# Neighbourhood attention beside dense products: four units under way, a single gate tile, longer beginnings

## The chip, the cores and the metric

The kernel runs on one core of a Trainium2 chip. The metric is the device time of one execution in microseconds (us), median over the runs. The profile is of one execution on the same chip.

## The reference

One encoder layer on two sequences (1024 and 2048 tokens of 1024 features) with 16 meta tokens ahead of each. All in fp32.

```python
xn = _rmsnorm(h, g_pre)
proj = xn @ w_in + b_in                       # 1024 x 6672
na_q, na_k, na_v, na_z, ml_qk, ml_v, ml_z, ml_o, ml_g, mg = split(proj)
ya = neighbourhood_attention(na_q, na_k, na_v, na_rpb)   # 8 heads of 64, 8x16 windows on a 64-wide grid, plus meta tokens
ya = (ya * silu(na_z)) @ w_a
yb = (mlstm(ml_qk, ml_v, ml_g, ml_o, conv_w, head_g) * silu(ml_z)) @ w_b   # both directions, 4 heads of 128, head norm
ga, gb = split(sigmoid(mg))
y = (ga * ya + gb * yb) @ w_out
return h + _rmsnorm(y, g_post)
```

## The kernel before

Every fp32 product is made as three products of split operands (high by high, high by low, low by high), so most of TensorE's time goes into the dense projections, at lines 144 to 146 (512 columns wide), 394 to 396 and 1284 to 1286 (256 wide).

**Two generators.** `dense` yields the projections in pieces: groups of the input projection first, and then, for each block of 512 tokens (two of sequence 0, four of sequence 1), `final`: the products with `w_a` and `w_b` (L1258, through `mm3` at L144 to L146), gated by tiles `tg` that come from memory by DMA (L1247, multiplied in at L1263), and the product with `w_out` (L1284 to L1286). `sparse` yields, in the order mLSTM 0, attention 0, mLSTM 1, attention 1, the short dependent steps. `run` meters one against the other: after each step of `sparse`, which yields a figure in us (`A_NA` = 1.52 in attention, `A_N` = 1.85 in the mLSTM's norm), it takes so many us worth of products from `dense`:

```python
acc += w
while acc > 0.0:
    d = next(dense, None)
    if d is None or d is True:
        acc = 0.0
        break
    acc -= d
```

So a pause (`yield A_NA`) puts 1.52 us worth of products behind the step on TensorE. `dense` yields `True` while the next block is not ready, that is while its attention is not done; then the sparse steps follow one another with no product between. When `sparse` is over, what is left of `dense` runs.

**Order.** TensorE's instructions stand as they are written. On the other engines and on SP, which issues the DMAs, a scheduler sets the order; each engine then works strictly in that order.

**Attention** (`na`). For each of its heads (row block, pair `pr`, half `hh`), `na_prep` loads and splits the operands in six steps: DMAs for `qr`, `kr`, and for the first head of a pair `vr` and the gate `zt` (L613); then copies and subtractions on ScalarE and VectorE (`stk`, `qB`, `kd`, `kx`, `vt`). The first head's six steps come ahead of all scores, with one pause behind each. A head has four units `cb`. In step `u` of the loop: `na_scores` of unit u (two products into `sc` at L644 and L645, bias and maximum L648 on VectorE, exp L652 on ScalarE); pause; `na_scale` of unit u (L660, L661), and `na_out` of unit u-2 (four products of `vt` and `pts` at L681, then L685 and L687; behind the last unit of a pair the gating with `zt` at L689 and the store `ya` at L690); pause; `na_turn` of unit u-1 (four transposes at L669, then `pts` high on ScalarE, L671, and low on VectorE, L672); pause. Three units are under way at a time.

**Norm** (`ml_norm`). Loads of 256 tokens ahead (`hn`, `tog`, `szg`), statistics and normalisation on VectorE (L1158 to L1173), then transposes at L1184. One pause stands behind the first load.

**Between blocks.** `yload` reads the eight slices of the next block (`yr`, L1225: four from the attention's stores `ya`, four from the mLSTM's `yb`) and splits them into `yh` (L1227, ScalarE) and `yl` (L1228, VectorE). It is begun beside the `w_out` products of the block before as soon as the next block is ready, and at the block's start otherwise.

Of the kernel before, what the change touches and what calls it, by code (L numbers as in the profile page):

```python
# [9 lines left out]
F32 = mybir.dt.float32  # L10
F32R = mybir.dt.float32r
# [6 lines left out]
P = 128  # L18
# [30 lines left out]
def _row_types(R):  # L49

    out = []
    for t in range(R // 8):
        if t == 0:
            out.append((0, 0, 11))
        elif t == R // 8 - 1:
            out.append((2, R - 12, 12))
        else:
            out.append((1, 8 * t - 4, 15))
    return out
# [48 lines left out]
A_NA, A_D, A_A, A_N, A_G = 1.52, 1.63, 1.63, 1.85, 1.3  # L108


class K:
# [420 lines left out]
    def na(self, s, rts):  # L532

        tc, nc, i = self.tc, self.nc, self.i
        rows = _row_types(SEQLEN[s] // 64)
        with tc.tile_pool(name=f"na{s}{rts[0]}", bufs=1, side="right", reuse_waits="tile") as np_:
            self.qB = [np_.tile([P, 4, P], F32R, name=f"qB{j}") for j in range(2)]
            self.kx = [np_.tile([P, 16, 64], F32R, name=f"kx{j}") for j in range(2)]
            self.gts = [np_.tile([P, 17, 48], F32, name=f"gt{j}") for j in range(2)]
            for q in self.qB:  # L540
                nc.gpsimd.dma_start(q[64:128], i["onehot"].rearrange("a (b c) -> a b c", b=4))
            for g in self.gts:
                nc.gpsimd.memset(g[:, 0, :], 0.0)
                nc.gpsimd.memset(g[:, 16, :], 0.0)
            heads = [(rt, pr, hh) for rt in rts for pr in range(4) for hh in range(2)]
            n = len(heads)
            prep = self.na_prep(np_, s, rows, heads, 0)
            for k in range(6):
                next(prep, None)
                yield A_NA  # L550
            self.na_bias(rows, heads, 0)
            cur, nxt = self.head, None
            units = [(j, cb) for j in range(n) for cb in range(4)]
            ready = {}
            for u in range(len(units) + 2):
                if u < len(units):
                    j, cb = units[u]
                    if cb == 0:
                        cur = self.head
                        prep = self.na_prep(np_, s, rows, heads, j + 1) if j + 1 < n else iter(())  # L560
                        next(prep, None)
                    ready[u] = [cur, heads[j], cb, None, None, self.gts[j % 2]]
                    self.na_scores(np_, ready[u], rows)
                    if j + 1 < n and cb == 0:
                        self.na_bias(rows, heads, j + 1)
                yield A_NA
                if u < len(units):
                    self.na_scale(np_, ready[u])
                    if cb:
                        next(prep, None)  # L570
                if u >= 2:
                    self.na_out(np_, ready.pop(u - 2), s)
                yield A_NA
                if 1 <= u <= len(units):
                    self.na_turn(np_, ready[u - 1], rows)
                    if u < len(units) and cb >= 2:
                        next(prep, None)
                yield A_NA
# [9 lines left out]
    def na_prep(self, np_, s, rows, heads, j):  # L588

        nc, i = self.nc, self.i  # L590
        rt, pr, hh = heads[j]
        typ, lo, nr = rows[rt]
        ns, h0 = nr + 1, hh * 64
        ms, rs = ((nr, 0), (nr, 0), (0, 1))[typ]
        qr = np_.tile([P, 512], F32, name="qr", bufs=1)
        stk = np_.tile([P, 4, P], F32R, name="stk", bufs=2)
        qb = self.qB[hh]
        self.twice(qr, self.NQ[s][pr], h0, rt * 512)
        sv = stk.rearrange("p b t -> p (b t)")
        kr = np_.tile([P, 16, 64], F32, name="kr", bufs=1)  # L600
        kd = np_.tile([P, 16, 64], F32R, name="kd", bufs=2)
        kx = self.kx[hh]
        self.twice(kr[:, rs:rs + nr, :].rearrange("p a b -> p (a b)"), self.NK[s][pr], h0, lo * 64)
        self.twice(kr[:, ms, :], self.NKM[pr], h0, 0)
        ks = 8 * ns
        if hh == 0:
            self.vr = np_.tile([P, 8, P], F32, name="vr", bufs=1)
            f0 = pr * P
            nc.sync.dma_start(self.vr[ms * 8:ms * 8 + 8], self.NVM[:, f0:f0 + P].rearrange("(b c) f -> c b f", c=8))
            nc.sync.dma_start(self.vr[rs * 8:(rs + nr) * 8],  # L610
                              self.NV[s][:, lo * 8:(lo + nr) * 8, f0:f0 + P].rearrange("b q f -> q b f"))
            self.zt = np_.tile([P, 512], F32, name="zt", bufs=2)
            nc.sync.dma_start(self.zt, self.NZ[s][pr][:, rt * 512:(rt + 1) * 512])  # L613
            self.yg = np_.tile([P, 512], F32, name="yg", bufs=2)
        vr, zt, yg = self.vr, self.zt, self.yg
        if j < 2 or rows[heads[j - 2][0]][0] != typ:
            nc.gpsimd.dma_start(kx[64:128, :ns, :].rearrange("p a b -> p (a b)"), i["masks"][typ, :, :ns * 64])
        yield
        nc.scalar.activation(sv, qr, AF.Copy)
        yield  # L620
        nc.scalar.activation(qb[0:64], stk[0:64].bitcast(F32), AF.Copy)
        nc.vector.tensor_tensor(sv[64:128], qr[64:128], sv[64:128].bitcast(F32), op=ALU.subtract)
        yield
        nc.scalar.activation(kd[:, :ns, :], kr[:, :ns, :], AF.Copy)
        yield
        nc.vector.tensor_tensor(kx[0:64, :ns, :], kr[0:64, :ns, :], kd[0:64, :ns, :].bitcast(F32), op=ALU.subtract)
        vt = np_.tile([P, 8, 2, 64], F32R, name="vt", bufs=2)
        vv = vr[:ks, :, h0:h0 + 64]
        nc.scalar.activation(vt[:ks, :, 0], vv, AF.Copy)
        yield  # L630
        nc.vector.tensor_tensor(vt[:ks, :, 1], vv, vt[:ks, :, 0].bitcast(F32), op=ALU.subtract)
        self.head = stk, qb, kd, vt, yg, zt
        yield

# [28 lines left out]
    def na_turn(self, np_, unit, rows):  # L663
        nc = self.nc
        pr_, _, N = unit[3]
        ks = N // 4
        pt = self.psum("tr", [P, 4, P])
        for ch in range(4):
            nc.tensor.transpose(pt[:ks, ch, :], pr_[:, ch * ks:(ch + 1) * ks], self.ident)  # L669
        pts = np_.tile([P, 4, 2, P], F32R, name="pts", bufs=2)  # L670
        nc.scalar.activation(pts[:ks, :, 0, :], pt[:ks], AF.Copy)  # L671
        nc.vector.tensor_tensor(pts[:ks, :, 1, :], pt[:ks], pts[:ks, :, 0, :].bitcast(F32), op=ALU.subtract)  # L672
        unit[4] = pts
# [461 lines left out]
    def ml_norm(self, mp, s):  # L1135

        nc = self.nc
# [3 lines left out]
        def load(i):  # L1141
            if i < N:
                ld[i] = []
                for e in range(2):
                    rows = slice((2 * i + e) * P, (2 * i + e + 1) * P)
                    hb = mp.tile([P, 4, P], F32, name="hn", bufs=6)
                    to = mp.tile([P, 4, P], F32, name="tog", bufs=4)
                    sz = mp.tile([P, 4, P], F32, name="szg", bufs=4)
                    for x, dr in ((hb, self.H), (to, self.TO), (sz, self.SZ)):
                        nc.sync.dma_start(x.rearrange("p a b -> p (a b)"), dr[s][rows, :])  # L1150
                    ld[i].append((hb, to, sz))
# [38 lines left out]
                rr.pop(i)  # L1190

        load(0)
        yield A_N
        for i in range(N + 1):
            if i < N:
                load(i + 1)
# [272 lines left out]
```

## Time and profile before

| what | value |
|---|---|
| median of 3 runs | 2956.09 us (2948.89 to 2957.51) |
| the profiled execution | 2951.54 us, of it a span of 2949.8 us |
| TensorE busy | 2837.0 us, 96% |
| VectorE busy | 1788.2 us, 61% |
| ScalarE busy | 1322.5 us, 45% |
| mean granted clock of TensorE | 0.991 |

The span runs from the first to the last instruction. PE is TensorE, DVE is VectorE, ACT is ScalarE, SP the queue that issues the DMAs. The norm and attention stages that matter below lie at about 713 to 775 us (norm 0), 776 to 1178 us (attention 0), 1908 to 2004 us (norm 1) and 2007 to 2830 us (attention 1); the final blocks run from 2230 us on. "PE sm L681 <- DVE pts L672: 24.9, 23, 2.6" in the view of waits reads: TensorE sat idle ahead of line 681, whose output is `sm`, until VectorE's line 672 had written `pts`: 24.9 us in all, 23 times, the longest 2.6 us. A row of the windows gives the stretch, its length, the busy time and number of instructions of PE, PEld, DVE, ACT and POOL, and then TensorE's granted clock, the DMA's busy share and GB/s.

### The profile page before, as it was taken

How to read it: one execution, taken by the hardware profiler on the slowest of the kernel's cores; microseconds unless marked ns; L12 is line 12 of the kernel's file. 1: busy time of each engine (PE TensorE's matmuls, PEld its weight loads, DVE VectorE, ACT ScalarE, POOL GpSimd, SP SyncE). 2: the span in 40 equal slices, each digit the busy share in tenths (PEclk: the TensorE clock that was granted, in tenths of full speed). 3: DMA queues.
4: the chain of work that ended last, by engine and by line, in shares of the span. 5: the costliest groups of instructions: out<-in, count | busy, mean ns of one | idle time of the engine just before them, and what ended most of it. 6: DMA issues, size and time to landing. Idle time of an engine off the chain costs nothing. (4 is left out here: it accounts for less than half of the span.)

```text
span 2949.8 us, 49769 instructions
## 1 busy us (share of the span) xinstructions
PE 2837.0 (96%) x17616; PEld 2520.4 (85%) x17616; DVE 1788.2 (61%) x4818; ACT 1322.5 (45%) x3178; POOL 23.5 (1%) x111
## 2 busy tenths in 40 slices
PE   6999999999999999999999999999999989999998
PEld 6998897899799988888888988877887978888897
DVE  5233566556656764565566565495568877776853
ACT  4113545433443453455565454434455544544421
POOL 1000000000000000000000000000000000000000
PEclk9999999999999999999999999999999999999999
DMA  7555666556756563666765554496579898988875
GB/s 252 199 176 183 204 212 204 166 176 210 237 176 197 152 189 101 203 193 194 222 206 189 173 182 151 160 356 196 179 232 329 288 276 268 281 273 252 287 260 205
DMA packets 415914, 633.33 MB, mean 215 GB/s; under 512 B 51920, under 2 KB 252704, under 8 KB 415664
## 3 DMA queue, kind: packets, MB, share of 16 engines
q1 hardware_dynamic: 414544, 627.46, 66.7%
q0 software_dynamic: 1120, 2.69, 0.4%
q8 instruction: 138, 2.26, 0.3%
q14 instruction: 112, 0.92, 0.1%
HBM read 438.27 MB, written 191.74 MB: 214 GB/s over the span
## 5 line engine op out<-in xcount | busy, mean ns | idle before, releaser
L144 PE MATMUL pj<-xh,whi 128*128 128x512 f32 (+1 forms) x1824 | 722.4, 396 | 1.2 <-DVE xl L299 0.9
L145 PE MATMUL pj<-xl,whi 128*128 128x512 f32 (+1 forms) x1824 | 701.9, 385 | 0.1
L146 PE MATMUL pj<-xh,wlo 128*128 128x512 f32 (+1 forms) x1824 | 700.2, 384 | 0.0
L394 PE MATMUL pj<-whi,xh 128*128 128x256 f32 (+3 forms) x1576 | 450.9, 286 | 0.0
L395 PE MATMUL pj<-wlo,xh 128*128 128x256 f32 (+3 forms) x1576 | 444.6, 282 | 0.0
L396 PE MATMUL pj<-whi,xl 128*128 128x256 f32 (+3 forms) x1576 | 444.0, 282 | 0.0
L146 PEld LDWEIGHTS pj<-xh,wlo 128*128 128x128 f32 x1824 | 345.2, 189 | 72.3
L144 PEld LDWEIGHTS pj<-xh,whi 128*128 128x128 f32 x1824 | 345.9, 190 | 57.6 <-DVE xl L299 1.3
L145 PEld LDWEIGHTS pj<-xl,whi 128*128 128x128 f32 x1824 | 346.1, 190 | 53.7 <-DVE xl L299 0.4
L394 PEld LDWEIGHTS pj<-whi,xh 128*128 128x128 f32 (+1 forms) x1576 | 294.1, 187 | 1.2
L395 PEld LDWEIGHTS pj<-wlo,xh 128*128 128x128 f32 (+1 forms) x1576 | 293.8, 186 | 1.1
L396 PEld LDWEIGHTS pj<-whi,xl 128*128 128x128 f32 (+1 forms) x1576 | 293.9, 186 | 0.9
L1284 PE MATMUL pj<-whi,mh 128*128 128x256 f32 x768 | 220.1, 287 | 0.6 <-DVE yo L1312 0.6
L652 ACT ACTIVATE prb<-sc,mx 128x384 f32<-128x384 f32 (+2 forms) x192 | 119.5, 622 | 220.1 <-DVE mx L648 211.4
L1286 PE MATMUL pj<-whi,mlo 128*128 128x256 f32 x768 | 216.4, 282 | 0.0
L1285 PE MATMUL pj<-wlo,mh 128*128 128x256 f32 x768 | 216.2, 281 | 0.0
L672 DVE TENSOR_TENSOR pts<-tr,pts 96x512 fp32r<-96x512 f32 (+2 forms) x192 | 131.9, 687 | 120.6 <-ACT pts L671 119.6
L671 ACT ACTIVATE pts<-tr 96x512 fp32r<-96x512 f32 (+2 forms) x192 | 114.5, 596 | 153.2 <-PE tr L669 152.3
L144 PE MATMUL pj<-yh,whi 128*128 128x512 f32 x384 | 158.0, 411 | 19.8 <-DVE tg L1263 19.8
L403 DVE TENSOR_TENSOR stT<-pj,bb 128x256 f32<-128x256 f32 (+3 forms) x197 | 83.0, 422 | 123.5 <-PE pj L396 121.7
L146 PE MATMUL pj<-yh,wlo 128*128 128x512 f32 x384 | 153.0, 398 | 0.0
L145 PE MATMUL pj<-yl,whi 128*128 128x512 f32 x384 | 152.8, 398 | 0.0
(234 smaller groups left out, 5145.0 us busy)
## 6 DMA issues: line engine op xcount, KB each, us to landing
whi<-wh SPq DMA_DIRECT2D x176, 512.0 KB
wlo<-wl SPq DMA_DIRECT2D x176, 512.0 KB
wh<-whi SPq DMA_DIRECT2D x64, 512.0 KB
wl<-wlo SPq DMA_DIRECT2D x64, 512.0 KB
wraw<-w_in SPq DMA_DIRECT2D x48, 512.0 KB
gt<-st SPq DMA_DIRECT2D x96, 256.0 KB
tg<-gt SPq DMA_DIRECT2D x96, 256.0 KB
xr<-x_sample SPq DMA_DIRECT2D x24, 512.0 KB
```

The source lines that it names most:

```text
L144: mm(out, ah, bh, start=start, stop=False)
L145: mm(out, ah, bl, start=False, stop=False)
L146: mm(out, al, bh, start=False, stop=stop)
L394: nc.tensor.matmul(o, xh, wh, start=k == 0, stop=False)
L395: nc.tensor.matmul(o, xh, wl, start=False, stop=False)
L396: nc.tensor.matmul(o, xl, wh, start=False, stop=k == KT - 1)
L652: nc.scalar.activation(pr_[:, :N].rearrange("p (b a c) -> p b a c", b=4, c=8), sc[:, :N].rearrange("p (a b c) -> p b a c", b=4, c=8), AF.E ...
L671: nc.scalar.activation(pts[:ks, :, 0, :], pt[:ks], AF.Copy)
L672: nc.vector.tensor_tensor(pts[:ks, :, 1, :], pt[:ks], pts[:ks, :, 0, :].bitcast(F32), op=ALU.subtract)
L1284: nc.tensor.matmul(o, mh[:, k, xs], wh, start=k == 0, stop=False)
L1285: nc.tensor.matmul(o, mh[:, k, xs], wl, start=False, stop=False)
L1286: nc.tensor.matmul(o, ml[:, k, xs], wh, start=False, stop=k == KT - 1)
```

## The change

Four edits. `na_out` comes three steps behind the scores instead of two, and `pts` gets three buffers for it. `zt` is loaded at the end of the second head's preparation, into one buffer instead of two, and held by the head rather than by `self`. In `na`, three pauses instead of one stand behind the first step of the first preparation, which issues the loads. In `ml_norm`, four pauses instead of one stand behind the first load. The products are the same in number and order; the attention's and the norm's instructions stand at other places among them.

```diff
             for k in range(6):
                 next(prep, None)
-                yield A_NA
+                for _ in range(1 if k else 3):
+                    yield A_NA
...
-            for u in range(len(units) + 2):
+            for u in range(len(units) + 3):
...
-                if u >= 2:
-                    self.na_out(np_, ready.pop(u - 2), s)
+                if u >= 3:
+                    self.na_out(np_, ready.pop(u - 3), s)
                 yield A_NA
...
-            self.zt = np_.tile([P, 512], F32, name="zt", bufs=2)
-            nc.sync.dma_start(self.zt, self.NZ[s][pr][:, rt * 512:(rt + 1) * 512])
             self.yg = np_.tile([P, 512], F32, name="yg", bufs=2)
-        vr, zt, yg = self.vr, self.zt, self.yg
+        vr, zt, yg = self.vr, None, self.yg
...
         nc.vector.tensor_tensor(vt[:ks, :, 1], vv, vt[:ks, :, 0].bitcast(F32), op=ALU.subtract)
+        if hh:
+            zt = np_.tile([P, 512], F32, name="zt", bufs=1)
+            nc.sync.dma_start(zt, self.NZ[s][pr][:, rt * 512:(rt + 1) * 512])
         self.head = stk, qb, kd, vt, yg, zt
...
-        pts = np_.tile([P, 4, 2, P], F32R, name="pts", bufs=2)
+        pts = np_.tile([P, 4, 2, P], F32R, name="pts", bufs=3)
...
         load(0)
-        yield A_N
+        for _ in range(4):
+            yield A_N
         for i in range(N + 1):
```

## The prediction

> **What bounds the kernel now.** I read the busy shares first, then the chain of waits of TensorE, then windows around each long wait.
>
> ```profile
> span 2949.8 us, 49769 instructions
> PE 2837.0 (96%) x17616; PEld 2520.4 (85%) x17616; DVE 1788.2 (61%) x4818; ACT 1322.5 (45%) x3178; POOL 23.5 (1%) x111
> ```
>
> TensorE (PE) is the bound: 2837.0 of 2949.8 us are busy, 112.8 us idle. The change keeps every matrix product, so it can only move idle time. The profiled execution took 2951.54 us, 1.7 us beside its span, and lies 4.6 us under the median 2956.09 of the three runs; I work the sum on the profile and carry the difference to the median. A measurement of this kernel tells about 0.3% (8.9 us) from no change.
>
> The waits of TensorE over the whole span (us in total, times, longest):
>
> ```profile
> PE sm L681 <- DVE pts L672: 24.9, 23, 2.6
> PE pj L144 <- DVE tg L1263: 19.8, 7, 5.4
> PE tr L1184 <- DVE hn L1173: 5.2, 1, 5.2
> PE sc L644 <- ACT kd L624: 3.8, 1, 3.8
> PE tr L1184 <- issue: 2.8, 1, 2.8
> PE sc L645 <- DVE kx L626: 0.5, 1, 0.5
> ```
>
> The edits aim at L681 (the attention's last product waits for the turned probabilities, `pts`), at L1184 (the first transposes of a norm, twice) and at L644/L645 (first scores of an attention). The direct cause of L1263 stays: VectorE waits for the gate tiles `tg`, which come by DMA.
>
> An idle stretch costs more than itself. Windows behind such waits (the last figures of a row are granted clock, DMA share, GB/s):
>
> ```profile
> 735.00:742.00 7.00, 5.76 (x19) 4.82 (x20) 7.00 (x32) 1.19 (x2) 0.00 (x0) 0.53 0.56 191
> 786.00:793.00 7.00, 6.46 (x17) 5.05 (x17) 2.00 (x4) 1.15 (x2) 0.00 (x0) 0.51 1.03 354
> 1018.00:1021.50 3.50, 3.50 (x19) 3.49 (x19) 2.90 (x8) 1.69 (x5) 0.00 (x0) 0.52 0.00 0
> 2629.20:2632.60 3.40, 3.40 (x12) 2.70 (x11) 2.94 (x7) 1.88 (x4) 0.00 (x0) 0.50 0.89 285
> 1928.00:1935.00 7.00, 7.00 (x34) 5.70 (x33) 7.00 (x37) 1.85 (x3) 0.00 (x0) 1.00 1.03 405
> ```
>
> After the norm's 5.2 us wait (it ends at 736.2) the clock is 0.53 for 7 us: 3.3 us lost. After the first scores' 4.3 us it is 0.51 for 7 us: 3.4 us. After two of the L681 waits it is half for 3.4 to 3.5 us: 1.7 us each. After the second norm's 2.8 us wait it stayed 1.00.
>
> **The fourth unit.** `na_out` of a unit moves behind one more step of three pauses, each metered as 1.52 us of products: 4.56 us more between the write of `pts` and its use. The longest of the 23 waits is 2.6 us, so all are covered: 24.9 us, and 1.7 us of clock twice, 28.3 us. `pts` gets a third buffer; its slot is still freed one step before it is written again, so no new wait. `vt` of the head before is read one step later, which leaves one step before it is overwritten: nothing, as long as `na_out` is on time.
>
> How much is given back? Most of these waits lie beside the final blocks. The waits from 2230 to 2800 us, of TensorE and then of VectorE:
>
> ```profile
> PE sm L681 <- DVE pts L672: 19.8, 20, 2.6
> PE pj L144 <- DVE tg L1263: 17.4, 5, 5.4
> ...
> DVE tg L1263 <- DMA tg<-gt: 30.6, 21, 4.3
> ```
>
> And that stage in windows:
>
> ```profile
> 2240.00:2380.00 140.00, 131.06 (x830) 114.85 (x828) 120.23 (x266) 75.88 (x169) 0.00 (x0) 1.00 0.94 306
> 2380.00:2520.00 140.00, 127.76 (x806) 112.95 (x807) 106.57 (x251) 64.17 (x154) 0.00 (x0) 0.99 0.89 274
> 2520.00:2660.00 140.00, 127.11 (x805) 113.55 (x803) 104.20 (x247) 63.59 (x154) 1.02 (x2) 0.98 0.89 270
> 2660.00:2800.00 140.00, 135.32 (x875) 122.38 (x876) 110.75 (x268) 66.95 (x164) 0.00 (x0) 0.99 0.84 274
> ```
>
> L681 has 19.8 of its 24.9 us here, next to 17.4 us that go back to late `tg`. DMA is busy for 0.84 to 0.94, VectorE for 74% to 86%: neither is full on the mean, both are near it in bursts. A PE that waits less asks for transfers sooner. The give-back lies between 0 and all 21.5 us (19.8 and 1.7 of clock); with 6 to 16% of DMA free I take 8 us.
>
> On the clock, the Trainium skill ("TensorE: Matmul & The Clock Gate", Part 1: The HAM clock gate) says that the array falls to half rate after at least one idle window of about 3.4 us. The trace disagrees as to the length: the L681 wait ahead of the third window above was shorter,
>
> ```profile
> 1016.88 0.39 PE L681 MATMUL sm<-pts,vt 104*128 104x256 f32 x1 [2.25 <-DVE pts L672]
> ```
>
> 2.25 us. By that page the L681 waits would cost no clock, and the sum would be 3.4 us smaller. I go by the trace.
>
> **The beginnings.** A norm gets three more pauses of 1.85 us, 5.55 us of products against waits of 5.2 and 2.8 us: both go, 8.0 us, and 3.3 us of clock: 11.3. The two attentions get 3.04 us after the first loads; only the first waits there, 4.3 us: 3.0 us go, 1.3 us stay, too short to drop the clock (2.8 us did not in the second norm): 6.4 us. If transfers rather than time end these waits, the gain shrinks to nothing; that is a rival below.
>
> **The gate tile.** `zt` is loaded into one buffer at the end of the odd head's preparation instead of with the even head. On SP it can go out once the pair before has been multiplied (L689), and it stands behind that pair's store `ya`, whose wait is the same one. Its use is some seven units, about 30 us, later: nothing. If that cover were gone, L689 would hold VectorE for the load, 2.8 us by the `yr` row below (issue 2832.59, use 2835.39).
>
> **The end, where the change costs.** More pauses mean more products used up: 2x2x1.52 + 2x3x1.52 + 2x3x1.85 = 26.3 us. Before, the last attention product was followed by products in stock. The timeline of that place:
>
> ```profile
> 2824.76 0.60 PE L669 MATMUL tr<-ident,prb 128*104 128x128 f32 x4
> 2825.45 0.60 ACT L671 ACTIVATE pts<-tr 104x512 fp32r<-104x512 f32 x1 [1.62 <-PE tr L669]
> 2826.09 0.69 DVE L672 TENSOR_TENSOR pts<-tr,pts 104x512 fp32r<-104x512 f32 x1 [1.46 <-ACT pts L671]
> 2828.04 0.63 PE L681 MATMUL sm<-pts,vt 104*128 104x256 f32 x4
> 2828.51 0.28 PE L1284 MATMUL pj<-whi,mh 128*128 128x256 f32 x1
> ...
> 2829.65 0.69 DVE L689 TENSOR_TENSOR yg<-yg,zt 128x512 f32<-128x512 f32 x1
> 2830.37 0.32 SPq L690 DMA_DIRECT2D ya<-yg  x1
> 2832.59 0.32 SPq L1225 DMA_DIRECT2D yr<-ya  x1
> 2834.85 1.19 SPq L231 DMA_DIRECT2D wlo<-wl  x2
> 2835.39 0.63 ACT L1227 ACTIVATE yh<-yr 128x512 fp32r<-128x512 f32 x1 [1.92 <-DMA yr<-ya]
> 2836.06 0.69 DVE L1228 TENSOR_TENSOR yl<-yr,yh 128x512 fp32r<-128x512 f32 x1 [2.13 <-ACT yh L1227]
> 2837.15 0.42 SPq L1225 DMA_DIRECT2D yr<-yb  x1
> 2846.19 0.69 DVE L1228 TENSOR_TENSOR yl<-yr,yh 128x512 fp32r<-128x512 f32 x1 [3.70 <-ACT yh L1227]
> 2847.06 0.40 PE L144 MATMUL pj<-yh,whi 128*128 128x512 f32 x1
> 2847.30 0.39 PE L145 MATMUL pj<-yl,whi 128*128 128x512 f32 x1
> ```
>
> From 2828.51 to 2847.06 PE had 18.6 us of products, under which the last `yg` was stored, read back as `yr` and split into `yh`, `yl`. 26.3 exceeds 18.6 by 7.7 us, five pauses. The order of the changed program's instructions says the same: no product stands between the last four transposes and the last block, and the last two `na_out` stand back to back. So that chain is bare. From the transposes (time 0) `pts` is ready at 2826.78 - 2824.76 = 2.0; PE has 0.9 us of work, waits 1.1, and starts the last `na_out` at 2.0, ending at 2.5. From its start to the fourth `yl`, which is made from this store, takes 2836.75 - 2828.04 = 8.7 us: 10.7. The first three slices are ready earlier, and their nine products run meanwhile, 9 x 0.235 = 2.1 us, to 4.6: wait 6.1 us. The eighth `yr` waits for the slot of the fourth, so its `yl` comes 2.8 + 1.4 us after the fourth's, at 14.9, against twelve products from 10.7, 2.8 us: wait 1.4 us. Some Newton steps stand between on VectorE (I allow 0.5), and half clock may follow: 1.7 to 3.4 us. Lower end 1.1 + 6.1 + 1.4 + 0.5 = 9.1. Upper end: the eighth `yr` lands as late as before (2846.88 - 2828.04 = 18.8 us after the last `na_out` starts, weights were ahead of it), so 20.8 - 2.5 - 21 x 0.235 = 13.4, with 1.1 and 3.4: 17.9. In the changed order the weights go out ahead of `ya`, so I take 12, nearer the lower.
>
> **Sum.** -28.3 + 8 - 11.3 - 6.4 + 12 = -26.0 us: the profile 2951.5 becomes 2925.5, the median 2956.1 becomes 2930.
>
> **Rivals.**
> *The final blocks are full.* The 21.5 us there come back as waits for `tg`: -46.0 + 21.5 + 12 = -12.5, 2943.6. For it: DMA at 0.94. Against: 2660 to 2800 has the smallest share, 0.84, and the least idle PE. Chance 0.23.
>
> *The beginnings don't do what they say.*
>
> ```profile
> 725.00:736.50 11.50, 6.25 (x28) 4.80 (x27) 10.42 (x59) 5.39 (x10) 0.00 (x0) 0.93 1.01 383
> ```
>
> Ahead of the first norm's transposes VectorE is busy 10.42 of 11.5 us and DMA is full; added products bring their own evacuations and weights there. Then only the fourth unit counts: -28.3 + 8 + 12 = -8.3, 2947.8. Against: the wait comes once and not again in the norm. Chance 0.12.
>
> *Slower: late gate tiles multiply.* Attention shifts against the final blocks, so each head's loads meet other `tg` loads. A late one costs up to 5.4 us and 1.7 of clock, 7 us. To eat the 34 us of net gain before give-back and 8.9 more it takes over six such waits, one more in each of the six blocks; at seven, +15 us, 2971. For it: five in the stage already. Against: nothing makes them more frequent. Chance 0.13.
>
> **How the numbers follow.** The forecast keeps 0.52. Its best case is -46.0 + 9.1 = -37 us, 2919, and the runs spread 7 us below their median: 2912. Above, the range takes in the first two rivals with 5 us: 2953; it leaves out the third. Faster: 0.50 + 0.18 + 0.04 = 0.72; same 0.02 + 0.05 + 0.08 = 0.15; slower 0.13.
>
> **What would show it.** Right: L681's wait below 5 us; no wait over 2 us at L1184; a PE gap of 6 to 13 us between the last attention product and the last block, with half clock behind it; `tg` waits of 20 to 30 us. Wrong: `tg` waits over 40 us, or L681's wait turned up at L644 or L669, or an end gap over 18 us.

## The result: 0.5% slower, and the profile after

| kernel | median | runs | ratio to before (95%) |
|---|---|---|---|
| before | 2954.94 us | 4 (2948.89 to 2957.51) | |
| changed | 2970.89 us | 4 (2968.22 to 2972.52) | 1.0050 [1.0028, 1.0071] |

The changed kernel is 16 us slower; the forecast was 2930 with a range of 2912 to 2953. The profiled execution took 2972.22 us against 2951.54. Its page:

```profile
span 2970.5 us, 49826 instructions
PE 2849.1 (96%) x17616; PEld 2531.6 (85%) x17616; DVE 1790.1 (60%) x4818; ACT 1324.3 (45%) x3178; POOL 23.3 (1%) x111
```

The products are the same 17616, yet TensorE is busy for 12.1 us longer than before (2837.0), at a mean granted clock of 0.984 for 0.991, and idle for 121.4 us instead of 112.8. TensorE's waits over the whole span of the changed kernel (us in total, times, longest), those that the argument uses:

```profile
PE pj L144 <- DVE tg L1266: 18.0, 8, 4.6
PE pj L296 <- DVE xl L299: 14.9, 13, 2.9
PE pj L1289 <- DVE mlo L1270: 12.3, 5, 4.4
...
PE pj L144 <- ACT yh L1230: 6.5, 1, 6.5
PE sc L646 <- ACT kd L623: 6.0, 1, 6.0
PE tr L671 <- DVE prb L663: 5.0, 5, 1.6
...
PE sm L683 <- DVE pts L674: 1.0, 1, 1.0
```

L683 is the old L681: 24.9 us have become 1.0. The 8.0 us at L1184 are gone altogether. So of the three groups of waits that the edits aimed at two went as forecast, and the third, ahead of the first scores, did not. In their place stand L1289 (a `w_out` product waits for `mlo`, 0 before), 6.5 us at the last block's start, a longer wait ahead of the first scores (6.0 for 3.8), more at L671 (5.0 for 0.5) and, behind ScalarE's `prb`, at L646 (8.7 for 3.9), and more at L296, the transposes of the projection's input (7.6 before).

Where the time went is best read at equal products: the start of the product with the same number among those written into `pj`, in both traces, so that a stage is compared with the same stage. The gain or loss of each stage against before, in us (stages by their times in the kernel before; minus is faster):

| kernel | to 743: start, norm 0 | to 1109: attention 0 | to 1958: mLSTM 1, first half of norm 1 | to 2031: rest of norm 1 | to 2245: attention 1 alone | to 2838: beside final blocks | end | sum |
|---|---|---|---|---|---|---|---|---|
| forecast | -8.5 | -13.2 | -2.8 | 0 | 0 | -13.5 | +12 | -26.0 |
| changed | -9.9 | -5.8 | +7.3 | +4.5 | +2.8 | +7.8 | +14.0 | +20.7 |
| a1_unit | -3.6 | -5.9 | +16.4 | +6.7 | -3.3 | -3.0 | +5.0 | +12.4 |
| a2_pauses | -11.5 | -2.1 | +12.9 | -1.0 | +5.9 | +14.3 | +16.6 | +35.0 |
| a3_stock | -9.6 | -7.7 | +8.4 | +2.6 | -0.3 | -1.8 | +3.5 | -4.9 |
| a4_phase | -9.8 | -2.6 | +0.1 | -2.6 | +2.5 | -14.7 | +9.4 | -17.7 |
| b1_norm | -10.2 | -7.5 | +15.5 | +6.0 | -2.4 | -12.1 | +10.2 | -0.5 |
| b2_three | -11.5 | -2.6 | +4.2 | -0.5 | +2.3 | -10.8 | +3.6 | -15.2 |
| b3_best | -8.7 | -4.1 | -2.7 | -2.6 | -1.0 | -11.5 | +1.8 | -28.7 |
| b4_bare | -0.5 | -1.1 | +4.7 | -1.6 | +1.4 | -1.1 | +17.4 | +19.3 |
| c1_pool | -9.0 | -9.0 | +8.7 | +3.9 | -0.1 | +8.1 | +17.6 | +20.2 |
| c2_three_stock | -10.4 | -2.5 | +8.0 | -0.6 | +2.4 | -11.6 | +3.3 | -11.4 |
| c3_place | -0.8 | -0.9 | -1.6 | +2.3 | -3.0 | -17.0 | +3.6 | -17.2 |
| c4_bestpool | -9.9 | -0.2 | -1.3 | -2.6 | +2.0 | -17.1 | +1.0 | -28.0 |
| d1_nogate | -8.3 | -6.9 | +7.7 | +3.6 | +3.1 | -32.0 | +11.3 | -21.5 |
| d2_ml | +0.8 | -5.3 | +25.8 | +5.1 | -1.8 | +3.7 | +3.0 | +31.3 |
| d3_late | +0.2 | -1.7 | -1.0 | +1.1 | +6.7 | +9.2 | +1.4 | +16.0 |
| d4_place_nogate | -0.2 | -4.7 | +1.3 | -0.1 | -4.4 | -26.7 | +4.1 | -30.8 |
| d5_before_nogate | -2.4 | -2.0 | +6.4 | +2.3 | -4.6 | -26.2 | -2.9 | -29.4 |

Each row is one profiled execution; the last 69 us of attention 0 stand in the third column. How far one stage wanders by itself shows where two kernels are alike: b4_bare is the kernel before up to the last row block, and differs by 4.7 us in mLSTM 1. A single figure below 5 us is therefore not read. The changed kernel and b1_norm are alike up to norm 1, and there they agree: from 1109 to 1918 us they lose 12.1 and 14.2 us. The 8.2 us between their two figures of that stage arise in norm 1, whose pauses differ. So the changed kernel's +7.3 is 12.1 us lost before norm 1 and 4.9 gained in its first half.

Beside the final blocks the two kernels wait about equally long. The changed kernel from 2230 to 2830 us:

```profile
PE pj L144 <- DVE tg L1266: 15.7, 5, 4.6
PE pj L1289 <- DVE mlo L1270: 12.3, 5, 4.4
PE tr L671 <- DVE prb L663: 5.0, 5, 1.6
PE pj L1287 <- ACT mh L1269: 2.8, 3, 2.0
PE pj L1287 <- DVE tg L1266: 1.3, 1, 1.3
PE sc L646 <- ACT prb L654: 0.7, 1, 0.7
...
DVE tg L1266 <- DMA tg<-gt: 29.0, 24, 3.2
```

That is 37.8 us of TensorE's waits, where before had 39.4 (2230 to 2800 us), 19.8 of them at L681. VectorE's wait for gate tiles hardly moved: 29.0 us for 30.6. The clock did move. The windows of 560 us, of before and then of the changed kernel (the last three figures: granted clock, DMA share, GB/s):

```profile
2240.00:2800.00 560.00, 521.24 (x3313) 463.74 (x3312) 441.76 (x1029) 270.59 (x640) 1.02 (x2) 0.99 0.89 281
```

```profile
2240.00:2800.00 560.00, 524.65 (x3312) 470.95 (x3311) 439.15 (x1020) 270.81 (x639) 1.02 (x2) 0.97 0.90 283
```

Before's waits at L681 were 20 of 1 us on the mean; the changed kernel has the same time in 20 waits where before had 30, and its clock is 0.97. In the traces of 2230 to 2830 us the clock was half for 34.1 us, and for 13.7 before. If half of that time counts as lost, some 10 us more are lost in the changed kernel, by which an estimate of waits and clock together gives 55 us for it and 46 for before. That is near the 7.8 us that this stage lost. The same estimate gives 29 us for c3_place below (24.3 us of waits, 10.2 us at half clock), whose stage gained 17.0.

### The profile page after: what moved, and what is told of

Same layout as the page of the kernel before. It is cut to its first block, busy times and chain, and to the rows that moved or that the text cites. A ratio compares the mean times of both kernels' runs of the same rounds, so it can differ in the third digit from the quotient of the medians.

```text
span 2970.5 us, 49826 instructions
## 1 busy us (share of the span) xinstructions
PE 2849.1 (96%) x17616; PEld 2531.6 (85%) x17616; DVE 1790.1 (60%) x4818; ACT 1324.3 (45%) x3178; POOL 23.3 (1%) x111
## 4 chain that ended last, share of the span: by engine, by line
PE 77%; DMA 11%; DVE 7%; ACT 2%; issue 1%; SPq 1%; DVEq 0%; ACTq 0%
PE pj L144 13%; PE pj L145 13%; PE pj L146 13%; PE pj L394 6%; PE pj L395 6%; PE pj L396 6%; DMA tg<-gt 3%; PE pj L1289 3%; PE pj L1287 3%; PE pj L1288 3%; PE sm L683 2%; PE tr L671 2%; DMA um<-ud 2%; PE sc L646 1%; PE sc L647 1%
## 5 line engine op out<-in xcount | busy, mean ns | idle before, releaser
L144 PE MATMUL pj<-xh,whi 128*128 128x512 f32 (+1 forms) x1824 | 722.7, 396 | 1.3 <-ACT st L323 1.2
L144 PEld LDWEIGHTS pj<-xh,whi 128*128 128x128 f32 x1824 | 346.4, 190 | 58.1 <-ACT st L323 1.7
L1289 PE MATMUL pj<-whi,mlo 128*128 128x256 f32 x768 | 219.1, 285 | 12.3 <-DVE mlo L1270 12.3
L144 PE MATMUL pj<-yh,whi 128*128 128x512 f32 x384 | 160.0, 417 | 24.5 <-DVE tg L1266 18.0
L1289 PEld LDWEIGHTS pj<-whi,mlo 128*128 128x128 f32 x768 | 147.5, 192 | 13.3 <-DVE mlo L1270 13.3
```

The lines of the kernel that those rows point to most:

```text
L144: mm(out, ah, bh, start=start, stop=False)
L1289: nc.tensor.matmul(o, ml[:, k, xs], wh, start=False, stop=k == KT - 1)
```

## The experiments

In all of them "place" is how many us of products the metering has handed out when a step begins. Before, mLSTM 1 begins at 951.8 and attention 1 at 1624.9, and 18.6 us of products are left in stock when the last attention is over. In the changed kernel it is 964.5, 1643.2 and none.

**a1_unit: the fourth unit alone.** The changed kernel without the two edits of pauses:

```diff
-                for _ in range(1 if k else 3):
-                    yield A_NA
+                yield A_NA
...
-        for _ in range(4):
-            yield A_N
+        yield A_N
```

> The fourth unit (with pts in three buffers and the gate tile in one) without any of the added pauses. It uses 9.1 us more products than the kernel before, so about 10 of the 18.6 us of stock behind the last attention product stay. Theory (the end and the shifted beginnings cost, the unit alone gives nothing in the final blocks): L681's waits below 3 us, but the waits in the final blocks turn up at the w_out product that needs the last low half of m (12 us) and at the transposes (5 us); norm waits as before (8 us); end gap below 5 us; time within 6 us of before, 2949 to 2961. Rival (the deeper pipeline itself is what slows the kernel): within 4 us of the changed kernel, 2967 to 2975. My prediction's view: 20 us faster than before, 2935.

Measured: 2962.55 us (10 runs), 1.0023 [1.0008, 1.0037], just over the theory's 2961 and 27 us above the prediction's 2935. The unit moves mLSTM 1 to 956.0 and attention 1 to 1629.1; that stage lost 16.4 us. So the unit without the pauses was no gain either.

**a2_pauses: the pauses alone, three units.** The kernel before with both edits of pauses.

> The added pauses of attention and norm alone; three units as before. 17.2 us more products are used, so the stock at the end is all but gone. Theory (the end costs 11 us, the norm's waits go for 11 us): L681 waits stay near 25 us; no wait at L1184; a gap at the start of the last block of 4 to 8 us with half clock behind it; time 2952 to 2966. Rival (the pauses are harmless, the unit is what costs): 2938 to 2948.

Measured: 2986.05 us, 1.0104 [1.0076, 1.0132]. Both expectations missed: alone, the pauses cost 29 us beside a median before of 2957.1. With three units in this place L682 (the old L681) waits longer than before. From 2230 to 2850 us:

```profile
PE sm L682 <- DVE pts L673: 36.4, 19, 6.1
PE pj L144 <- DVE tg L1265: 6.6, 2, 4.8
PE tr L670 <- DVE prb L662: 2.9, 2, 1.8
```

**a3_stock: the end restored by faster attention 1.** The changed kernel with attention 1's pauses metered as 1.454, so that the stock at the end is 18.6 again.

```diff
+        a_na = (A_NA, 1.454)[s]
...
-                yield A_NA
+                yield a_na
```

> The changed kernel with the second attention's pauses metered at 1.454 us instead of 1.52, so that the stock of products at the end is again that of the kernel before (18.6 us). Theory (the bare end costs 1.0 + 6.5 us of gap and 3.4 us of half clock): the last block starts without a gap; 11 us faster than the changed kernel, 2957 to 2963. Rival (the end is only where a delay from earlier shows, because the last attention unit came late anyway): under 4 us faster, 2967 or more.

Measured: 2945.50 us, 0.9960 [0.9946, 0.9974], more than expected. The end fell from +14.0 to +3.5, as the theory had it; the final blocks fell too, by 9.6 us. The smaller pauses also move every head, which may be why; it was not tested apart.

**a4_phase: mLSTM 1 back at its place.** The changed kernel with attention 0's pauses as 1.459: mLSTM 1 begins at 951.8 as before, attention 1 at 1630.5, and TensorE has 5.8 us of products behind the last attention product (3 were expected).

```diff
+        a_na = (1.459, A_NA)[s]
...
-                yield A_NA
+                yield a_na
```

> The changed kernel with the first attention's pauses metered at 1.459 us, so that the second mLSTM begins at the same place among the products as in the kernel before; the end has 3 us of stock. Theory (the 12.8 us shift puts the transposes that build the next half beside heavier mLSTM steps): waits at L296 fall from 14.9 to about 8 us, the 12 us lost from 1484 to 1577 us don't come; 10 to 16 us faster than the changed kernel, 2955 to 2961. Rival (the transposes wait because VectorE's order is another with four units or norms, not for the place): waits at L296 stay at 13 to 16 us, time 2965 or more.

Measured: 2932.32 us, 0.9926 [0.9903, 0.9950]: 39 us below the changed kernel, with all its instructions and some shorter pauses. The theory gave 10 to 16. mLSTM 1's stage went from +7.3 to +0.1, the final blocks from +7.8 to -14.7.

**b1_norm: only attention 1 at that place.** The changed kernel with norm 1's pauses as 1.580: mLSTM 1 stays at 964.5, attention 1 begins at 1631.9.

```diff
+        a_n = (A_N, 1.580)[s]
...
-            yield A_N
+            yield a_n
```

> The changed kernel with the second norm's pauses metered at 1.580 us instead of 1.85: the second mLSTM keeps the shifted place among the products, the second attention begins within 2 us of products of where it begins in the version with the first attention metered (2932 us), and the stock at the end is the same 3 us. It parts the two shifts. Theory (each shift has its own price: 12 us at the second mLSTM, some 22 us in the final blocks): L296 waits near 15 us as in the changed kernel, final blocks as in the faster version; time 2940 to 2950. Rival (only the mLSTM's place matters, the final blocks were a matter of luck): 2955 to 2965. Other rival (only the final blocks' place matters): 2930 to 2936.

Measured: 2947.43 us, 0.9972 [0.9953, 0.9990], as the theory had it: the final blocks gain (-12.1), mLSTM 1's stage still loses (+15.5).

**b2_three: that place with three units.** The kernel before with the changed kernel's pauses, attention 0's as 1.4775: the places of a4_phase, 10 us in stock.

> Three units and the gate tile as before, the added pauses, and the first attention metered at 1.4775 us so that the second mLSTM and the second attention begin at the same place among the products as in the version at 2932 us; 10 us of stock at the end against its 3. It isolates the fourth unit at one place. Prediction's term (L681's waits and their clock are worth 28 us, 8 of it given back): 18 to 28 us slower than 2932, 2950 to 2960, L681 waits 20 us or more. Rival (in the final blocks the waits only move to the transposes and the low half of m, the unit is worth the 6 us of the first attention): 2930 to 2940.

Measured: 2936.31 us, 0.9942 [0.9921, 0.9962]. The rival was right: 2936 with three units, 2932 with four. The waits of the final blocks, 2230 to 2830 us, are about equal in sum, 25.2 us here and 24.5 in a4_phase (beside 3.9 at the start of its last block), and differ in where TensorE meets them:

```profile
PE sm L683 <- DVE pts L674: 19.8, 16, 3.1
PE pj L144 <- DVE tg L1266: 2.8, 2, 2.4
PE pj L1287 <- ACT mh L1269: 1.8, 1, 1.8
```

```profile
PE tr L672 <- DVE prb L664: 10.3, 11, 2.0
PE pj L1288 <- ACT mh L1270: 4.8, 3, 2.0
PE pj L144 <- ACT yh L1231: 3.7, 2, 3.5
PE pj L1290 <- DVE mlo L1271: 3.2, 4, 1.6
```

The first fence is b2_three, the second a4_phase.

**b3_best: a4_phase with products in stock for the end.** The last row block's pauses as 1.37, by which 21.5 us of products stand behind the last attention product (18.7 were expected):

```diff
+                    if s and heads[j][0] == 3:
+                        a_na = 1.37
```

> The version at 2932 us with the last row block's pauses metered at 1.37 us, so that 18.7 us of stock stay behind the last attention product. Theory (a bare end costs 7 to 13 us): the 9.4 us lost there don't come, 2920 to 2927, the fastest so far. Rival (the place in the last block but one counts more): 2930 or more.

Measured: 2923.52 us, 0.9896 [0.9866, 0.9926], the theory's figure and the fastest complete kernel here: 1% below the one before.

**b4_bare: the bare end alone.** The kernel before with the last row block's pauses as 1.714, so that no product is left in stock.

> The kernel before with nothing changed but the last row block's pauses, metered at 1.714 us, so that no product is in stock behind the last attention product. It measures the bare end by itself. Theory: a gap of 5 to 8 us at the start of the last block with half clock behind it, 8 to 16 us slower than before. Rival (the end hides it): within 4 us of before.

Measured: 2964.55 us, 1.0036 [1.0014, 1.0059]; 10 us slower, the end +17.4 in the profiled execution, which took 2970.88. The term of the forecast for the end is real by itself.

**c1_pool: is VectorE's burst the carrier?** The changed kernel with one line on another engine:

```diff
-                nc.vector.tensor_tensor(yl[:, k - 2], yr.pop(k - 2), ...)
+                nc.gpsimd.tensor_tensor(yl[:, k - 2], yr.pop(k - 2), ...)
```

> The changed kernel with one operation moved: the subtraction that makes yl for the next block (L1231) runs on GpSimd instead of VectorE; every instruction keeps its place among the products. It asks what carries the waits in the final blocks. Theory: bursts of VectorE do (four yl and the gating of yo stand ahead of the mlo or the turned probabilities that TensorE needs), so without yl in that queue the waits at L1289 fall from 12.3 us to under 5, those at L671 fall too, and the time is 8 to 12 us below the changed kernel: 2959 to 2963. Rival: late gate tiles or the place of the mLSTM carry the loss; then the waits change by less than 4 us in all and the time stays at 2967 or more.

Measured: 2968.94 us, 1.0045 [1.0032, 1.0057], 2 us below the changed kernel: the theory fell. From 2230 to 2830 us the waits moved again:

```profile
PE pj L144 <- DVE tg L1266: 20.9, 7, 4.7
PE pj L1289 <- DVE mlo L1270: 8.0, 4, 2.8
PE tr L671 <- DVE prb L663: 5.9, 5, 1.8
PE sc L646 <- ACT prb L654: 3.9, 4, 1.6
PE pj L1287 <- ACT mh L1269: 1.6, 1, 1.6
```

40.3 us in all. VectorE was relieved by 16.5 us only (below), so the test was weaker than meant, but what it did free bought nothing: the final blocks lost 8.1 us, as in the changed kernel.

**c2_three_stock: the fourth unit by itself at the good place.** b3_best with three units; pauses 1.4775 and, in the last row block, 1.432, give the same places and nearly the same stock (20.1 us for 21.5).

> The kernel b3_best with three units under way instead of four (and pts and zt in two buffers as before); its pauses give the same places for the mLSTM and the attention and the same stock at the end. It measures the fourth unit by itself at a good place. Theory: the unit only moves the waits of the final blocks from L681 to other lines and is worth 8 us at most: 2926 to 2932. Rival, the prediction's term (28.3 us of waits and clock gone, 8 given back): about 20 us above b3_best, 2943 or more.

Measured: 2935.28 us, 0.9945 [0.9924, 0.9965], between the two expectations: the two kernels lie 11.8 us apart. How much of it is the unit's stays open: the two traces differ most in mLSTM 1's stage (by 10.7 us), which holds no attention, and not at all beside the final blocks (-11.6 and -11.5).

**c3_place: one edit of the kernel before.** Only norm 1's three pauses: attention 1 at 1630.5, mLSTM 1 unmoved, 13 us in stock.

```diff
-        yield A_N
+        for _ in range((1, 4)[s]):
+            yield A_N
```

> The kernel before with a single edit: three more pauses in the second norm (5.55 us of products). The mLSTM keeps its place among the products, attention 1 begins 5.6 us of products later, and 13 us of products stay in stock at the end. Theory: the place of attention 1 against the final blocks is worth 13 to 15 us by itself, beside some us from the norm's wait: 2938 to 2945. Rival: the place is worth nothing and only the norm's wait of 2.8 us goes: 2950 to 2956.

Measured: 2936.25 us, 0.9937 [0.9916, 0.9959]; 19 us, slightly more than the theory gave, for 5.6 us of products moved. Apart from norm 1's 2.8 us at L1184 the waits at which the change aimed are still there. In the final blocks the gate tiles' wait at L144 is the one that went, from 17.4 to 3.3. From 2230 to 2830 us:

```profile
PE sm L681 <- DVE pts L672: 21.0, 19, 2.5
PE pj L144 <- DVE tg L1264: 3.3, 2, 3.0
DVE tg L1264 <- DMA tg<-gt: 21.8, 17, 2.7
```

**c4_bestpool: b3_best with `yl` on GpSimd.**

> The kernel b3_best with the yl subtraction on GpSimd. Theory (VectorE's bursts carry what waits are left in the final blocks, some 15 us at L671, L1287 and L1289): 2915 to 2921. Rival: at this place the bursts no longer meet TensorE, or GpSimd's longer operation delays the next block's start; then 2923 or more.

Measured: 2926.75 us, 0.9907 [0.9885, 0.9929]: no gain over b3_best. The rival held.

**d2_ml: the place of mLSTM 1 alone.** The kernel before with attention 0's pauses as 1.582 and norm 1's as 1.553: mLSTM 1 at 964.5, attention 1 at 1624.9 as before.

> The kernel before with its pauses in attention 0 stretched from 1.52 to 1.582 and those in the second norm cut from 1.85 to 1.553: mLSTM 1 begins after 964.5 us of products as in the changed kernel, attention 1 after 1624.9 as before. It measures by itself what the later place of mLSTM 1 costs. Theory: 10 to 13 us, as the transposes that build half of the input operand for its groups meet VectorE late (waits at L296 for xl over 10 us, half clock near 1510 and 1553 us): 2962 to 2968. Rival: that loss belongs to the other edits of the changed kernel; then 2953 to 2958.

Measured: 2980.32 us, 1.0085 [1.0065, 1.0105]; 25 us slower, twice what the theory gave, and not at the line that it named: TensorE waits only 3.9 us for `xl` between 1100 and 1970 us. Of the stage's 25.8 us, 20.8 were lost before norm 1 (by 1918 us in the kernel before), in several small waits and three half clocks (near 1203, 1254 and 1524 us); the rest, and the 5.1 us behind it, belong to norm 1, whose pauses are cut. That the later place costs is shown here, and by b1_norm's +15.5 beside a4_phase's +0.1; which wait carries it differs from kernel to kernel. It is not the place alone: c2_three_stock, at the old place of 951.8, lost 8.0 us in this stage.

**d3_late: attention 1 at the changed kernel's place, else as before.** Ten more pauses in norm 1, attention 1 at 1643.2; the last row block as 1.385, 14 us in stock.

> The kernel before with ten more pauses in the second norm, 18.3 us of products: attention 1 begins after 1643.2 as in the changed kernel; mLSTM 1 keeps its place and the last row block's pauses are cut to 1.385 so that 14 us of products stay in stock at the end. With c3_place (1630.5, 2936 us) and the kernel before (1624.9, 2955 us) it shows whether the place of attention 1 has a good and a bad side. Theory: 1643.2 is as bad a place as 1624.9, with 35 us or more of waits between 2230 and 2830 us, and the time is 2948 to 2958. Rival: any later place is good, and the loss of the changed kernel comes from mLSTM 1 and its bare end alone: 2932 to 2942.

Measured: 2963.98 us (10 runs), 1.0022 [1.0008, 1.0037], on the theory's side and worse, with 40.6 us of TensorE's waits from 2230 to 2830 us. So with three units 1630.5 is good (2936), 1624.9 and 1643.2 are bad (2955 and 2964): it isn't that later is better. How wide the good place is stays open: a1_unit, with four units at 1629.1, gained only 3.0 us beside the final blocks.

**d1_nogate, d4_place_nogate and d5_before_nogate: no gate loads, at three places.** The changed kernel, c3_place and the kernel before, each with one load left out:

```diff
-                    nc.sync.dma_start(tg, self.GT[s][8 * br + ft][:, t0:t0 + n])
...
-                nc.vector.scalar_tensor_tensor(ms[br], ms[br], 1.0, p, ...)
+                nc.vector.scalar_tensor_tensor(ms[br], self.gpost[:, :n], 1.0, p, ...)
```

> The changed kernel without the loads of the gate tiles tg (the gating multiplies by a tile that is in memory already, so 24 MB of loads and the gating's values are left out); all instructions of TensorE keep their places. It asks whether late gate tiles carry the waits that the final blocks have at this place. Theory: they do, as the cause behind L144 and L1289 alike, so of the 38 us of waits between 2230 and 2830 us fewer than 18 stay and the time is 15 to 25 us below the changed kernel, 2946 to 2956. Rival, the one that c1_pool leaves standing for VectorE itself (whatever is taken away, its queue is met by TensorE at another line): at least 28 us of waits stay and the time is 2962 or more.

> The kernel c3_place without the loads of the gate tiles (left out as in d1_nogate). At this place only 3 us of TensorE's waits are for tg. Theory (the place acts by way of late gate tiles): little is left to gain, 0 to 6 us below c3_place, 2930 to 2937, with 18 to 22 us of waits at L681. Rival (gate loads slow everything beside them by the room they take on DMA): 10 us or more below, 2926 or less.

> The kernel before without the loads of the gate tiles (left out as in d1_nogate). With the changed kernel (2971 to 2925.5 without them) and c3_place (2936 to 2922.7) it completes the comparison of three places of attention 1. Theory (the place acts on the final blocks through the gate loads): the kernel before falls by 20 to 28 us, to 2927 to 2935, and in the final blocks it comes to within 6 us of c3_place without gate loads. Rival (the place acts by itself and the loads only add a constant 10 to 14 us): 2941 or more.

| attention 1 begins at | with gate loads | without | final blocks with / without |
|---|---|---|---|
| 1624.9 (before) | 2955 | 2923.28, 0.9891 [0.9866, 0.9917] | 0 / -26.2 |
| 1630.5 (c3_place) | 2936.25 | 2922.72, 0.9890 [0.9870, 0.9910] | -17.0 / -26.7 |
| 1643.2 (changed) | 2970.89 | 2925.48, 0.9902 [0.9882, 0.9922] | +7.8 / -32.0 |

With the loads the three lie 35 us apart, without them 3. Leaving them out takes 45 us off the changed kernel, twice what the theory gave; 30 to 32 off the kernel before, somewhat more than 28; and 13.5 off c3_place, which is more than the theory's 6 and on the side of the rival there. So the loads also add a cost of their own, 10 to 14 us even at the good place, and beyond it **the place of attention 1 acts on the final blocks through the gate loads**. The changed kernel differs from the other two also in its fourth unit and in mLSTM 1's place; before and c3_place differ in norm 1's pauses alone, and the 17.0 us between their final blocks become 0.5 without the loads. d1_nogate from 2230 to 2830 us (which takes in its end, the wait for `yh`), and its window:

```profile
PE pj L144 <- ACT yh L1230: 6.4, 1, 6.4
PE tr L671 <- DVE prb L663: 6.3, 5, 2.4
PE sc L646 <- ACT prb L654: 4.1, 2, 2.6
PE pj L1288 <- DVE mlo L1269: 3.5, 2, 2.7
PE sm L683 <- DVE pts L674: 1.0, 1, 1.0
```

```profile
2240.00:2800.00 560.00, 547.24 (x3615) 497.52 (x3614) 461.68 (x1086) 289.29 (x693) 1.02 (x2) 1.00 0.80 257
```

Not only the waits for `tg` at L144 are gone but most of those at `mlo` (12.3 to 3.5), and the clock is back at 1.00. The waits at L671 are not gone (6.3 for 5.0). VectorE works in order, so its wait for a gate tile holds all that stands behind it, and TensorE can meet it at a later line. Three things went with the loads and were not separated: the lateness of the tiles, the room that they take on DMA (0.90 to 0.80 without them), and their places in SP's queue ahead of other loads. Loading the tiles earlier, into more buffers, was not tried.

## Why the prediction was wrong, step by step

**The bound and two of the aimed waits: right.** TensorE's products are unchanged, L681 fell from 24.9 to 1.0, L1184 from 8.0 to 0. The single gate tile cost nothing, as forecast; VectorE's idle time ahead of its use, the last figure of this group of the changed kernel, is 0.2 us in all:

```profile
L691 DVE TENSOR_TENSOR yg<-yg,zt 128x512 f32<-128x512 f32 x24 | 16.4, 685 | 0.2
```

Of the signs of being wrong, `tg` waits over 40 us and an end gap over 18 us did not come. L681's wait turned up only in part at the old L644 and L669, which wait 4.8 and 4.5 us more for `prb`; most of it came at the `w_out` product behind `mlo`, which no sign named.

**The give-back in the final blocks: the mechanism was named, its size was not.** The forecast lets 21.5 us go there and 8 come back; measured is a loss of 7.8, so 21.3 us of the 46.7 between forecast and result. The step that failed took the give-back as a share of what was freed, 8 of 21.5 us. What came back is nearly all of the waits, 37.8 us for 39.4, and where the sum took 1.7 us of clock off, the estimate above has some 10 us more of it lost. Two things stand apart there. The waits at L681 have a cause of their own; without any gate load, d5_before_nogate still has, from 2230 to 2830 us:

```profile
PE sm L681 <- DVE pts L672: 17.0, 15, 2.5
```

With the loads present a fourth unit only moves them to other lines (25.2 and 24.5 us at a4_phase's place). And what late gate tiles cost depends on the place, not on what was freed: 39.8 us in the changed kernel's final blocks (+7.8 to -32.0), 26.2 before, 9.7 in c3_place. Without gate loads the changed kernel's final blocks are 5.3 to 5.8 us ahead of the three-unit kernels' (-32.0 against -26.7 and -26.2), little more than one stage wanders by itself. At fixed places the two comparisons of whole kernels give the four-unit kernel 4.0 us (b2_three and a4_phase) and 11.8 (c2_three_stock and b3_best).

**The place: missing from the sum.** The forecast counted the pauses' 26.3 us of products only at the end, where the stock runs out. The same 26.3 us move mLSTM 1 by 12.7 and attention 1 by 18.3 us of products, and that was costed at nothing. Attention 1's place alone is worth -19 us at 1630.5 (c3_place, norm 1's 2.8 us at L1184 among them) and +8 at 1643.2 (d3_late); mLSTM 1's alone +21 in its stage ahead of norm 1 (d2_ml). In the changed kernel that stage lost 7.3 us where the sum had a gain of 2.8, and ahead of norm 1 it lost 12.1. A half clock there belongs to a short wait at L296; its row of TensorE's timeline, and the window behind it:

```profile
1508.44 0.66 PE L296 MATMUL pj<-ident,xr 128*128 128x128 f32 x4 [1.94 <-DVE xl L299]
```

```profile
1509.10:1512.50 3.40, 3.40 (x11) 2.73 (x11) 1.79 (x5) 0.67 (x3) 0.00 (x0) 0.50 0.86 308
```

The third rival, "late gate tiles multiply", had the right carrier and the right cause (attention shifts against the final blocks), and got 0.13. That its sum gives the measured time, 2971, is luck: it needs seven more late tiles, while the number of waits for `tg` at L144 stayed at five there, and of the 46.7 us between forecast and result more than half lie in other stages. What it overlooked is that a late tile is met at `mlo` as well.

**The beginnings: half right.** The first norm gave what was forecast (-9.9 by 743 us, -8.5 expected). The first attention did not: its wait grew from 3.8 to 6.0. The scores and the first loads, in the kernel before and then in the changed one:

```profile
775.66 1.15 SPq L530 DMA_DIRECT2D qr<-nq  x2
785.67 0.44 PE L644 MATMUL sc<-kd,stk 128*128 128x384 f32 x1 [3.77 <-ACT kd L624]
```

```profile
776.72 1.14 SPq L530 DMA_DIRECT2D qr<-nq  x2
787.87 0.69 PE L646 MATMUL sc<-kd,stk 128*128 128x384 f32 x1 [5.97 <-ACT kd L623]
```

TensorE reached the scores at 781.9 in both, and the loads went out no earlier though TensorE was ahead by then: the loads rather than the products beside them end this wait, as the forecast's own condition for the beginnings and the second rival had it. What holds the loads was not isolated. Attention 0's stage brought 5.8 of the 13.2 us forecast. Norm 1's wait at L1184 went, but a wait of 2.9 us at L296 (at 1993.4, with half clock behind it) came in its second half, where nothing stood in the sum (+4.5 us, too little to be read by itself), and the second attention's scores wait 4.9 us at 2046.9.

**The end: right.** Forecast 12 us; measured is nearly the chain that was forecast, a wait of 1.0 at the last attention product, three slices' nine products, then 6.5 us (forecast 6.1), in all +14.0. TensorE at the end of the changed kernel:

```profile
2857.60 0.74 PE L683 MATMUL sm<-pts,vt 104*128 104x256 f32 x4 [1.00 <-DVE pts L674]
...
2860.01 0.39 PE L146 MATMUL pj<-yh,wlo 128*128 128x512 f32 x1
2866.92 0.80 PE L144 MATMUL pj<-yh,whi 128*128 128x512 f32 x1 [6.52 <-ACT yh L1230]
```

The doubled 0.80 for one product (0.39 above it) is half clock. The forecast second wait, for the eighth slice, does not show.

## What to carry to other kernels

Where one stream of work is metered against another, a pause changes the place of everything behind it: cost the shifted place for every later stage, or hold the places fixed (b3_best does it by trimming other pauses) and measure the edit alone. A wait at one line of an engine that runs strictly in order is often just where a common cause is met; before removing it, find what that engine itself waits for (here 30 us of VectorE for gate tiles) and price the cause by leaving its load out. If the sum of the waits stays and only their lines change, as here from 39.4 to 37.8 us, the cause is still there.

## What the hardware showed beside this

Short stretches of idleness can drop the clock. The wait of 1.94 us above was followed by 3.4 us at half rate; around the waits of 5.97 us (787.87) and 6.52 us (2866.92) the clock was half for 6.8 us each (785.5 to 792.3 and 2864.2 to 2871.0), beginning within the wait. Not every such wait does: the 2.8 us ahead of the second norm in the kernel before left the clock at 1.00. So waits of about equal sum went with a clock of 0.97 in the changed kernel and 0.99 before.

In c1_pool VectorE was slower where GpSimd worked beside it. There the 48 subtractions took 1.448 us each on GpSimd, against 0.687 on VectorE, and took 31.9 us off VectorE; but VectorE's busy time fell only by 16.5 us, from 1790.1 to 1773.6. Its groups of 2230 to 2850 us, changed kernel and then c1_pool (busy us, mean ns):

```profile
L1270 DVE TENSOR_TENSOR mlo<-tg,mh 128x512 fp32r<-128x512 f32 x39 | 26.6, 681 | 0.3
```

```profile
L1270 DVE TENSOR_TENSOR mlo<-tg,mh 128x512 fp32r<-128x512 f32 x39 | 30.0, 771 | 0.2
```

The multiplication out of PSUM, `tg` by `pj` at L1266, stayed at 682 ns. The Trainium skill ("GPSIMD Engine Reference", 1. Specifications) says that the two engines share their SBUF interfaces, and names VectorE's instructions with two inputs in SBUF among those that contend. These rows agree.
